# Seven products of a paced pair in two runs of matmuls, and a new order for ScalarE and VectorE

## The chip, the cores and the metric

The kernel runs on one core of one Trainium2 chip. The metric is device time in microseconds (us) of one execution, the median of several. Five engines of the core work side by side, each through its own list of instructions in order: TensorE (PE in the profile; its weight loads are listed apart as PEld), VectorE (DVE), ScalarE (ACT), GpSimd (POOL) and SyncE (SP, which only issues transfers here). They wait for one another by semaphores.

## What is computed

Two layers of a transformer on 512 tokens of width 1024, all in float32. Each layer has a feed-forward block, a token mixer, and a second feed-forward block, each followed by a layer norm. The change touches the first half of the feed-forward blocks only, of which there are four in the program:

```python
def _swiglu(x, w1, w2):
    gt, up = jnp.split(x @ w1, 2, axis=-1)
    return (jax.nn.silu(gt) * up) @ w2          # x: 512 x 1024, w1: 1024 x 5632, w2: 2816 x 1024

for l in range(DEPTH):                          # DEPTH = 2
    x = _layer_norm(DN_ALPHA * x + 0.5 * _swiglu(x, ffn1_w1[l], ffn1_w2[l]), ...)
    x = _layer_norm(DN_ALPHA * x + _token_mix(x, ...), ...)
    x = _layer_norm(DN_ALPHA * x + 0.5 * _swiglu(x, ffn2_w1[l], ffn2_w2[l]), ...)
```

`gt` and `up` have 2816 columns each, that is 22 blocks of 128. A **pair** is one such block of the gate columns with the same block of the up columns.

## The kernel before

**Split operands.** Every float32 operand stands as a high part (the value rounded to the type that TensorE multiplies in one pass) and a low part (the rest). A product is three matmuls: high by high, high by low, low by high. ScalarE makes the high part by a copy, VectorE the low part by a subtraction: lines 452 with `hi<-` and `lo<-` in the profile.

**Seven products.** Pairs 3 to 21 are computed by a scheme with seven half-size products in place of eight (Winograd's form), on sums of the tokens (tile `tz`, made once per block) and on sums of the weights (made for every pair). Pairs 4 to 21 go through `paced` (line 443), 18 iterations in each of the four blocks; these are the four **stages** of which this document speaks. Each product has contraction length 512, that is four steps of 128.

**sided** (line 411) issues products. Per product it issues four long matmuls (line 415: high weights by 512 columns, the high and low tokens side by side) and four short ones (line 418: low weights by 256 columns). Called with several products, it issues the long ones of all, then the short ones of all, these in reverse order if `back` is set. TensorE's order is that of the program text.

**The seven products of pair c, by letter** (weights in parentheses): P (`g1`) and Y (`g2`) use the two halves of the gate weights `ug`; D uses `ud`, the tile pair `dh`, `dl`; B (`ub`) and C (`uc`) use the two halves of the summed weights `u2`; A (`ua`) and E (`ue`) those of `u1`. P, B, A and E are summed one after the other in the PSUM bank `px`; D is summed into `pv`, Y into `py`, and C has `pc`. Between them stand copies by ScalarE: `px` after P goes to `py`, `px` after B to `pv`, `px` after A to the SBUF tile `cc`, and `px` after E, its second half, to `t`. Each copy must be done before the next product is added to `px`. VectorE then forms the up columns (`up`, line 505 and after: four additions on `cc` and `pv`), the gate columns (`gate`: two additions on `py` and `px`), ScalarE takes Silu of the gate, and VectorE multiplies the two.

**Weights of a pair.** `load` (line 470) fetches the raw gate and up columns, `rg` and `ru`, by SyncE. From them come `ug` = parts of `rg`; `dh`, `dl` = parts of the second half of `ru`; two sums in place in `ru` and in the tile `ws` (function `sums`); `u2` = parts of `ws`; `u1` = parts of `ru`. In the kernel before all of these are made for the **next** pair n, in the iteration of pair c.

**Order.** The helper `on` chains every instruction that `paced` gives to VectorE behind the one before it on VectorE, and the same on ScalarE. So each of the two engines takes the operations strictly in the order of the program text, and one that waits holds all behind it.

**Buffers.** `unit()` (line 143) hands out a pair of tiles `hi`, `lo` (1024 columns each), for `ug`, `u2` and `u1`. Successive calls go round a list of seven places in three pools; by the counter's value at the start of `paced` the pools come in the order wt, wt, wx, wx, w1p, w1p, wt, and again. The pool wt has three buffers, wx and w1p have two each. Within its pool a tile takes the buffer that came free first; where one alone is free or about to be, it takes that. It can be written only when the last reader of the buffer's former content is done. The same holds for the PSUM banks, which have four tags: `pc` and `px` of even iterations (counted from 0) share two banks; `px` of odd iterations and `pv` of even ones share two; `py` of even iterations has one; `pc`, `pv` and `py` of odd iterations share three.

Of the kernel before, what the change touches and what calls it, by code (L numbers as in the profile page):

```python
# [10 lines left out]
F32 = mybir.dt.float32  # L11
F32R = mybir.dt.float32r
BF = mybir.dt.bfloat16
AF = mybir.ActivationFunctionType
OP = mybir.AluOpType
# [4 lines left out]
P = 128  # L20
S, D, F = 512, 1024, 2816
KD, KF, NB = D // P, F // P, S // P
# [44 lines left out]
def body(tc, a, out, depth=DEPTH):  # L67
# [15 lines left out]
    def ps(tag=None, name="ps", shape=(P, 512)):  # L83
        if tag is None:
            tag = PS_ALL[ring[0] % 8]
            ring[0] += 1
        return psp.tile(list(shape), F32, name=name, tag=tag, bufs=PS_TAGS[tag])
# [29 lines left out]
    def wraw(shape=None):  # L117
        return wt.tile(list(shape or [P, KD, P]), F32, name="raw", tag="raw", bufs=3)
# [16 lines left out]
    def behind(*ins):  # L135

        st = ExitStack()
        for i in ins:
            if i:
                st.enter_context(tc.issue_after(i))  # L140
        return st

    def unit():

        if nx.pool:
            pl, nb = nx.pool, 4
        else:
            seq = [(wt, 3)] * 3 + [(more.pool, 2)] * 2 * bool(more.pool)
            if nx.w1:
                seq = seq[2:] + [(nx.w1, 2)] * 2 + seq[:2]  # L150
            more.n += 1
            pl, nb = seq[more.n % len(seq)]
        return [pl.tile([P, KD, P], F32R, name=n, tag=n, bufs=nb) for n in ("hi", "lo")]
# [193 lines left out]
    H1, H2 = slice(0, 256), slice(256, 512)  # L347
# [60 lines left out]
                nc.tensor.matmul(o, wx, vx, start=first and k == 0 and i == 0, stop=k == 3 and i == 2,  # L408
                                 skip_group_check=True)

    def sided(*ps_, back=False):
        for o, w, x, first in ps_:
            o = o.rearrange("p (z s) -> p z s", z=2)
            for k in range(4):
                nc.tensor.matmul(o, w[0][:, k], x[:, :, k], start=first and k == 0, stop=False, skip_group_check=True)  # L415
        for o, w, x, _ in reversed(ps_) if back else ps_:
            for k in range(4):
                nc.tensor.matmul(o[:, H1], w[1][:, k], x[:, 0, k], start=False, stop=k == 3, skip_group_check=True)  # L418

# [23 lines left out]
    def paced(w, c0, pl, tz, t2, hpart, fs, ws):  # L443

        last = {}
        V, A = nc.vector, nc.scalar

        def on(k, f, *args, **kw):  # L450
            with behind(last.get(k)), tc.high_priority(100):
                last[k] = f(*args, **kw).ins  # L452

        def tt(o, x, y, op=OP.add):
            on("v", V.tensor_tensor, o, x, y, op=op)

        def copy(o, x, f=AF.Copy):
            on("a", A.activation, o, x, f)

        def rest(lo, x, hi):  # L460
            tt(lo, x, hi.bitcast(F32), OP.subtract)

        v = w.rearrange("(k p) f -> p k f", p=P)
        h1, h2 = slice(0, 4), slice(4, 8)
        half = lambda u: [[y[:, h] for y in u] for h in (h1, h2)]
        two = lambda y: y.rearrange("p (z s) -> p z s", z=2)
        (t1, t2_, t3, t4) = [tz[:, i].rearrange("p k z s -> p z k s") for i in range(4)]
        p_, r_, s_ = [xx[:, :, k:k + 4, c] for k, c in ((0, H1), (4, H1), (4, H2))]

        def load(f):  # L470
            n = K()
            n.f, n.t, n.u = f, t2[:, f % 2], hpart(f)
            n.rg = wraw()
            nc.sync.dma_start(n.rg, v[:, :, f * P:f * P + P])
            n.ru = pl.tile([P, KD, P], F32, name="raw", tag="raw", bufs=2)
            nc.sync.dma_start(n.ru, v[:, :, c0 + f * P:c0 + f * P + P])
            return n

        def weights(n):
            n.dh, n.dl = [pl.tile([P, 4, P], F32R, name=x, tag=x, bufs=2) for x in ("dh", "dl")]  # L480
            n.wx = pl.tile([P, KD, P], F32, name="ws", tag="ws", bufs=1)
            n.ug, n.u2, n.u1 = unit(), unit(), unit()
            (a1, a2), (b1, b2) = half(n.u1), half(n.u2)
            n.ws = half(n.ug), (a2, b2, b1, a1), (n.dh, n.dl)

        def sums(n, i):
            if i == 0:
                rest(n.dl, n.ru[:, h2], n.dh)
                tt(n.ru[:, h2], n.ru[:, h1], n.ru[:, h2])
                rest(n.ug[1], n.rg, n.ug[0])  # L490
                g2 = n.rg[:, h1].rearrange("p k f -> p (k f)")[:, None].to_broadcast([P, 2, 512])
                tt(bk(n.wx), bk(n.ru), g2, OP.subtract)
            else:
                tt(n.ru[:, h1], n.rg[:, h2], n.wx[:, h2], OP.subtract)

        def gate(e, h, bank):
            tt(e.t[:, h], bank[:, H1], e.t[:, h])

        def up(e):
            m, side, c3 = e.cc[:, H1], e.cc[:, H2], e.cc[:, 512:768]  # L500
            tt(e.u[:, H2], m, side)
            tt(e.u[:, H1], e.pv[:, H1], c3)
            tt(e.u[:, H2], e.u[:, H2], c3)
            tt(e.u[:, H1], e.pv[:, H2], e.u[:, H1])

        bk = lambda y: y.rearrange("p (b k) f -> p b (k f)", b=2)
        fs = list(fs)
        c, e = K(), None
        c.f, c.t, c.u, c.ws = fs[0], t2[:, fs[0] % 2], hpart(fs[0]), ws
        n = load(fs[1])  # L510
        for _ in range(6):
            nc.vector.memset(ps(name="gap")[:, 0:1], 0.0)
        for f in fs:
            (g1, g2), (ua, ub, uc, _), ud = c.ws
            for x in (("pv", "py", "pc", "px"), ("pc", "pv", "py", "px"))[(f - fs[0]) % 2]:
                setattr(c, x, ps(name=x))
            first, b = (c.px, g1, p_, True), (c.px, ub, t2_, False)
            if e:
                copy(e.cc[:, 0:512], e.px)
            if e and e.f > fs[0]:  # L520
                sided((e.py, e.ws[0][1], r_, False), first, back=True)
            else:
                sided(first)
            if n:
                weights(n)
                copy(n.dh, n.ru[:, h2])
                copy(n.ug[0], n.rg)
                sums(n, 0)
            copy(c.py if e else c.t, c.px)
            if e:  # L530
                if e.f == fs[0]:
                    tt(e.t, e.py, e.t)
                    tt(e.t[:, H1], e.t[:, H1], e.t[:, H2])
                else:
                    copy(e.t[:, H1], e.py[:, H2])
                    gate(e, H1, e.py)
                sided((e.px, e.ws[1][3], s_, False), b, back=True)
            else:
                sided((c.py, g2, r_, True))
                sided(b)  # L540
            if n:
                sums(n, 1)
            copy(c.pv, c.px)
            if e:
                copy(e.t[:, H2], e.px[:, H2])
                up(e)
                gate(e, H2, e.px)
            sided((c.pc, uc, t3, True))
            if n:
                copy(n.u2[0], n.wx)  # L550
                rest(n.u2[1], n.wx, n.u2[0])
            if e:
                copy(e.t, e.t, AF.Silu)
                tt(e.u, e.t, e.u, OP.mult)
            if n:
                copy(n.u1[0], n.ru)
                rest(n.u1[1], n.ru, n.u1[0])
            c.cc = pl.tile([P, 1024], F32, name="cc", tag="cc", bufs=1)
            copy(c.cc[:, 512:768], c.pc[:, H2])
            tt(c.cc[:, 512:768], c.pc[:, H1], c.cc[:, 512:768])  # L560
            sided((c.pv, ud, t4, False), (c.px, ua, t1, False), back=True)
            e, c, n = c, n, load(f + 2) if f + 2 in fs else None
        copy(e.cc[:, 0:512], e.px)
        sided((e.py, e.ws[0][1], r_, False), (e.px, e.ws[1][3], s_, False))
        up(e)
        copy(e.t[:, H1], e.py[:, H2])
        gate(e, H1, e.py)
        copy(e.t[:, H2], e.px[:, H2])
        gate(e, H2, e.px)
        copy(e.t, e.t, AF.Silu)  # L570
        tt(e.u, e.t, e.u, OP.mult)
        return last["a"], last["v"]
# [1504 lines left out]
```

## Time and profile before

| what | us |
| --- | --- |
| median of three runs (2382.77 to 2385.82) | 2384.15 |
| the profiled execution's own time | 2385.5 |
| its span, from first to last instruction | 2383.5 |
| TensorE busy in the span | 2372.9 |
| VectorE busy | 2029.0 |
| ScalarE busy | 1380.6 |
| paced stages, from their first matmul on | 61.5 to 238.1, 910.1 to 1086.4, 1242.6 to 1418.9, 2090.6 to 2267.0 |

How to read a page: section 1 gives the busy time of each engine; section 4 follows the chain of work that ended last backwards, and gives its share by engine and line. The view by windows gives the busy time of each engine in a stretch. The timeline lists instructions in order: start, duration, engine, line, operation, out<-in, shapes, and in brackets the idle time just before it with the engine whose result ended it. Successive instructions of one engine overlap a little, so the distance between two starts, not the duration, is what one costs in a full queue. In the groups of four matmuls that the timeline merges, the distance from one group's start to the next is what the group costs.

### The profile page before, as it was taken

What the parts mean: (1) busy time and instruction counts of PE and PEld (TensorE: products, weight loads), DVE (VectorE), ACT (ScalarE), POOL (GpSimd) and SP (SyncE); (2) the same over time, 40 slices, a digit from 0 to 9 for tenths busy, and PEclk for the clock granted to TensorE, in tenths of its full rate; (3) what the DMA queues carried; (4) which work ended last, traced back from release to release, by engine and by line L of the source; (5) the groups of instructions that cost most, each with busy time, mean ns of one, the idle gap of its engine ahead of it and who ended that gap; (6) DMA issues with size and microseconds to landing.
All of it is one profiled execution on the core that took longest, in us unless ns stands there. A gap on an engine that the chain in (4) does not pass through costs nothing.

```text
span 2383.5 us, 38602 instructions
## 1 busy us (share of the span) xinstructions
PE 2372.9 (100%) x14017; PEld 2047.8 (86%) x14017; DVE 2029.0 (85%) x3974; ACT 1380.6 (58%) x2637; POOL 345.5 (14%) x598
## 2 busy tenths in 40 slices
PE   9999999999999999999999999999999999999998
PEld 8888888888889988888898888878888898888887
DVE  7999985787688889999799989667777888999996
ACT  4666644576644536666546666445766445466663
POOL 2000312133321000001100002122332210000021
PEclk9999999999999999999999999999999999999999
DMA  6433965633155353338833348645321654433394
GB/s 199 115 108 102 246 201 162 182 90 91 48 159 134 106 172 112 109 95 225 207 116 108 112 147 204 196 130 153 99 80 56 161 131 151 132 111 111 98 240 139
DMA packets 407933, 330.08 MB, mean 138 GB/s; under 512 B 19208, under 2 KB 349336, under 8 KB 407744
## 3 DMA queue, kind: packets, MB, share of 16 engines
q1 hardware_dynamic: 380752, 261.83, 37.0%
q0 software_dynamic: 26992, 65.80, 11.9%
q8 instruction: 110, 1.80, 0.3%
q14 instruction: 79, 0.65, 0.1%
HBM read 300.26 MB, written 17.88 MB: 133 GB/s over the span
## 4 chain that ended last, share of the span: by engine, by line
PE 99%; DMA 0%; DVE 0%; issue 0%; POOL 0%; SPq 0%; POOLq 0%; ACT 0%; DVEq 0%
PE acc L658 13%; PE px L415 11%; PE acc L195 7%; PE pj L181 6%; PE pj L183 6%; PE pj L182 6%; PE px L418 6%; PE pg L408 5%; PE py L415 3%; PE pv L415 3%; PE pc L415 3%; PE pu L408 2%; PE brp L181 2%; PE brp L182 2%; PE brp L183 2%; PE sN L1361 2%
## 5 line engine op out<-in xcount | busy, mean ns | idle before, releaser
L161 DVE TENSOR_TENSOR lo<-raw,hi 128x1024 fp32r<-128x1024 f32 x202 | 247.3, 1228 | 90.1 <-ACT hi L160 89.7
L160 ACT ACTIVATE hi<-raw 128x1024 fp32r<-128x1024 f32 x202 | 211.9, 1055 | 146.4 <-PE brp L182 36.3
L181 PE MATMUL pj<-xx,hi 128*128 128x512 f32 (+1 forms) x696 | 262.2, 377 | 1.8 <-ACT hi L1903 1.8
L183 PE MATMUL pj<-xx,lo 128*128 128x512 f32 (+1 forms) x696 | 251.0, 361 | 0.0
L182 PE MATMUL pj<-xx,hi 128*128 128x512 f32 (+1 forms) x696 | 250.7, 360 | 0.0
L658 PE MATMUL acc<-hi,xx 128*128 128x512 f32 x640 | 197.0, 389 | 0.0
L633 POOL DMA_DIRECT2D bt<-in_ffn_w_dram x32 | 40.3, 1266 | 924.7 <-DVE lo L161 712.3
L452 DVE TENSOR_TENSOR lo<-raw,hi 128x1024 fp32r<-128x1024 f32 x136 | 165.9, 1220 | 0.0
L415 PE MATMUL px<-tz,hi 128*128 128x512 f32 x576 | 156.8, 394 | 0.0
L415 PE MATMUL px<-xx,hi 128*128 128x512 f32 x576 | 156.0, 392 | 0.0
L183 PEld LDWEIGHTS pj<-xx,lo 128*128 128x128 f32 x696 | 131.9, 190 | 20.7 <-DVE lo L1904 0.2
L181 PEld LDWEIGHTS pj<-xx,hi 128*128 128x128 f32 x696 | 132.1, 190 | 17.8 <-issue 2.7
L182 PEld LDWEIGHTS pj<-xx,hi 128*128 128x128 f32 x696 | 132.4, 190 | 12.4 <-DVE xx L1989 0.2
L452 ACT ACTIVATE hi<-raw 128x1024 fp32r<-128x1024 f32 x136 | 142.6, 1048 | 0.1
L658 PEld LDWEIGHTS acc<-hi,xx 128*128 128x128 f32 x640 | 120.1, 188 | 25.0
L415 PEld LDWEIGHTS px<-tz,hi 128*128 128x128 f32 x576 | 107.2, 188 | 26.0 <-ACT py L452 2.3
L658 PE MATMUL acc<-lo,xx 128*128 128x512 f32 x320 | 124.5, 389 | 0.0
L415 PEld LDWEIGHTS px<-xx,hi 128*128 128x128 f32 x576 | 103.3, 189 | 18.2
L452 ACT ACTIVATE pv<-px 128x512 f32<-128x512 f32 x72 | 41.9, 582 | 124.7 <-PE px L418 124.7
L418 PEld LDWEIGHTS px<-tz,lo 128*128 128x128 f32 x576 | 88.1, 188 | 11.9
L418 PE MATMUL px<-xx,lo 128*128 128x256 f32 x576 | 92.0, 282 | 0.0
L418 PE MATMUL px<-tz,lo 128*128 128x256 f32 x576 | 91.3, 280 | 0.0
(490 smaller groups left out, 6776.9 us busy)
## 6 DMA issues: line engine op xcount, KB each, us to landing
raw<-in_ffn_w_dram SPq DMA_DIRECT2D x232, 512.0 KB, 3.9
raw<-in_w_in_dram SPq DMA_DIRECT2D x56, 512.0 KB, 4.1
raw<-in_w_gate_dram SPq DMA_DIRECT2D x48, 512.0 KB, 3.8
b<-in_ffn_w_dram SPq DMA_DIRECT2D x32, 512.0 KB, 6.7
bt<-in_ffn_w_dram POOLq DMA_DIRECT2D x32, 512.0 KB, 10.5
x_sp<-xa POOLq DMA_DIRECT2D x24, 512.0 KB, 6.1
xa<-x_sp POOLq DMA_DIRECT2D x24, 512.0 KB, 4.6
ks<-hl SPq DMA_DIRECT2D x96, 128.0 KB, 2.3
```

The costliest lines, as they stand in the source:

```text
L160: lnq.hi = nc.scalar.activation(hi[:, c], raw[:, c], AF.Copy).ins
L161: lnq.lo = nc.vector.tensor_tensor(lo[:, c], raw[:, c], hi[:, c].bitcast(F32), op=OP.subtract).ins
L181: nc.tensor.matmul(o, hi[:, k], vh, start=first, stop=False)
L182: nc.tensor.matmul(o, hi[:, k], vl, start=False, stop=False)
L183: nc.tensor.matmul(o, lo[:, k], vh, start=False, stop=last)
L195: nc.tensor.matmul(o, x(k)[:, t], y[:, c], start=first and i == 0, stop=last and i == 2, skip_group_check=True)
L408: nc.tensor.matmul(o, wx, vx, start=first and k == 0 and i == 0, stop=k == 3 and i == 2, skip_group_check=True)
L415: nc.tensor.matmul(o, w[0][:, k], x[:, :, k], start=first and k == 0, stop=False, skip_group_check=True)
L418: nc.tensor.matmul(o[:, H1], w[1][:, k], x[:, 0, k], start=False, stop=k == 3, skip_group_check=True)
L452: last[k] = f(*args, **kw).ins
L658: nc.tensor.matmul(o[t], u[:, k, s], v[:, c], start=first and j == 0 and i == 0, stop=False, skip_group_check=True)
L1361: nc.tensor.matmul(o[:, 0:nb].rearrange("p k b j -> p (k b j)"), q, kx[:, 2 * b0:2 * (b0 + nb)].rearrange("p a b -> p (a b)"), start=i == ...
```

## The change

`sided` takes for `back` the order in which the short matmuls are to follow. In an iteration there are now three pairs at work: c, the one before it e, and the one before that ee. From the third iteration on (index 2) TensorE issues two runs: the long matmuls of Y, D and A of e and of P of c (sixteen), then their short ones in the order A, P, D, Y; then the long ones of C of c, E of e and B of c (twelve), then the short ones in the order B, E, C. Before, there were four runs of eight, eight, four and eight long matmuls. Iterations 0 and 1 and the end of the loop have shorter forms.

The parts `u2` and `u1` are made for c in its own iteration, no longer for n in the one before; `ug`, `dh`, `dl` and the sums for n stay where the pair c is current. `unit()` is therefore called in each iteration for `ug` of n, `u2` of c and `u1` of c, in this order (iteration 0 only for `ug` of pair 1, and the last one only for `u2` and `u1`). The second half of the gate, Silu and the product of ee stand one iteration later than before.

VectorE's order in an iteration is now: gate of ee from `px`; the last sum of c; `lo` of `ug`; `lo` of `u2`; one addition on `cc` of e; `lo` of `u1`; the four additions of `up` of e; the product of ee; `dl` of n and a sum of n; gate of e from `py`; the sum in `ws` of n. ScalarE's is: `hi` of `ug`; copy `pc` to `cc` of e; `hi` of `u2`; `hi` of `u1`; Silu of ee; copy `px` to `cc` of e; copy `px` to `py` of c; copy `py` to `t` of e; `dh` of n; copy `px` to `pv` of c; copy `px` to `t` of e.

```diff
--- before.py
+++ after.py
@@ -408,12 +408,12 @@
                 nc.tensor.matmul(o, wx, vx, start=first and k == 0 and i == 0, stop=k == 3 and i == 2,
                                  skip_group_check=True)
 
-    def sided(*ps_, back=False):
+    def sided(*ps_, back=()):
         for o, w, x, first in ps_:
             o = o.rearrange("p (z s) -> p z s", z=2)
             for k in range(4):
                 nc.tensor.matmul(o, w[0][:, k], x[:, :, k], start=first and k == 0, stop=False, skip_group_check=True)
-        for o, w, x, _ in reversed(ps_) if back else ps_:
+        for o, w, x, _ in [ps_[i] for i in back] or ps_:
             for k in range(4):
                 nc.tensor.matmul(o[:, H1], w[1][:, k], x[:, 0, k], start=False, stop=k == 3, skip_group_check=True)
 
@@ -476,22 +476,32 @@
             nc.sync.dma_start(n.ru, v[:, :, c0 + f * P:c0 + f * P + P])
             return n
 
-        def weights(n):
-            n.dh, n.dl = [pl.tile([P, 4, P], F32R, name=x, tag=x, bufs=2) for x in ("dh", "dl")]
-            n.wx = pl.tile([P, KD, P], F32, name="ws", tag="ws", bufs=1)
-            n.ug, n.u2, n.u1 = unit(), unit(), unit()
-            (a1, a2), (b1, b2) = half(n.u1), half(n.u2)
-            n.ws = half(n.ug), (a2, b2, b1, a1), (n.dh, n.dl)
+        def parts(o, x):
+            copy(o[0], x)
+            rest(o[1], x, o[0])
 
         def sums(n, i):
             if i == 0:
+                n.dh, n.dl = [pl.tile([P, 4, P], F32R, name=x, tag=x, bufs=2) for x in ("dh", "dl")]
+                copy(n.dh, n.ru[:, h2])
                 rest(n.dl, n.ru[:, h2], n.dh)
                 tt(n.ru[:, h2], n.ru[:, h1], n.ru[:, h2])
-                rest(n.ug[1], n.rg, n.ug[0])
+            elif i == 1:
+                n.wx = pl.tile([P, KD, P], F32, name="ws", tag="ws", bufs=1)
                 g2 = n.rg[:, h1].rearrange("p k f -> p (k f)")[:, None].to_broadcast([P, 2, 512])
                 tt(bk(n.wx), bk(n.ru), g2, OP.subtract)
             else:
                 tt(n.ru[:, h1], n.rg[:, h2], n.wx[:, h2], OP.subtract)
+
+        def u2_parts(n):
+            n.u2 = unit()
+            parts(n.u2, n.wx)
+
+        def u1_parts(n):
+            n.u1 = unit()
+            parts(n.u1, n.ru)
+            (a1, a2), (b1, b2) = half(n.u1), half(n.u2)
+            n.ws = half(n.ug), (a2, b2, b1, a1), (n.dh, n.dl)
 
         def gate(e, h, bank):
             tt(e.t[:, h], bank[:, H1], e.t[:, h])
@@ -505,66 +515,95 @@
 
         bk = lambda y: y.rearrange("p (b k) f -> p b (k f)", b=2)
         fs = list(fs)
-        c, e = K(), None
+        def c_side(e):
+            e.cc = pl.tile([P, 1024], F32, name="cc", tag="cc", bufs=1)
+            copy(e.cc[:, 512:768], e.pc[:, H2])
+
+        def c_join(e):
+            tt(e.cc[:, 512:768], e.pc[:, H1], e.cc[:, 512:768])
+
+        def y_side(e):
+            if e.f > fs[0]:
+                copy(e.t[:, H1], e.py[:, H2])
+
+        def y_join(e):
+            if e.f > fs[0]:
+                gate(e, H1, e.py)
+            else:
+                tt(e.t, e.py, e.t)
+                tt(e.t[:, H1], e.t[:, H1], e.t[:, H2])
+
+        def prods(c):
+            (g1, g2), (ua, ub, uc, ue), ud = c.ws
+            return {"P": (c.px, g1, p_, True), "Y": (c.py, g2, r_, c.f == fs[0]), "B": (c.px, ub, t2_, False),
+                    "C": (c.pc, uc, t3, True), "D": (c.pv, ud, t4, False), "A": (c.px, ua, t1, False),
+                    "E": (c.px, ue, s_, False)}
+
+        c, e, ee = K(), None, None
         c.f, c.t, c.u, c.ws = fs[0], t2[:, fs[0] % 2], hpart(fs[0]), ws
         n = load(fs[1])
         for _ in range(6):
             nc.vector.memset(ps(name="gap")[:, 0:1], 0.0)
         for f in fs:
-            (g1, g2), (ua, ub, uc, _), ud = c.ws
             for x in (("pv", "py", "pc", "px"), ("pc", "pv", "py", "px"))[(f - fs[0]) % 2]:
                 setattr(c, x, ps(name=x))
-            first, b = (c.px, g1, p_, True), (c.px, ub, t2_, False)
+            if e is None:
+                sided(prods(c)["P"])
+                copy(c.t, c.px)
+            if ee:
+                gate(ee, H2, ee.px)
             if e:
+                sums(c, 2)
+            if n:
+                n.ug = unit()
+                parts(n.ug, n.rg)
+            if e:
+                c_side(e)
+                u2_parts(c)
+                c_join(e)
+                u1_parts(c)
+            if ee:
+                copy(ee.t, ee.t, AF.Silu)
+            q = prods(c)
+            if e:
+                r = prods(e)
+                if e.f > fs[0]:
+                    sided(r["Y"], r["D"], r["A"], q["P"], back=(2, 3, 1, 0))
+                else:
+                    sided(q["P"], r["D"], r["A"], back=(2, 0, 1))
                 copy(e.cc[:, 0:512], e.px)
-            if e and e.f > fs[0]:
-                sided((e.py, e.ws[0][1], r_, False), first, back=True)
-            else:
-                sided(first)
+                copy(c.py, c.px)
+                y_side(e)
+                up(e)
+            if ee:
+                tt(ee.u, ee.t, ee.u, OP.mult)
             if n:
-                weights(n)
-                copy(n.dh, n.ru[:, h2])
-                copy(n.ug[0], n.rg)
                 sums(n, 0)
-            copy(c.py if e else c.t, c.px)
             if e:
-                if e.f == fs[0]:
-                    tt(e.t, e.py, e.t)
-                    tt(e.t[:, H1], e.t[:, H1], e.t[:, H2])
-                else:
-                    copy(e.t[:, H1], e.py[:, H2])
-                    gate(e, H1, e.py)
-                sided((e.px, e.ws[1][3], s_, False), b, back=True)
-            else:
-                sided((c.py, g2, r_, True))
-                sided(b)
+                y_join(e)
             if n:
                 sums(n, 1)
+            if e:
+                sided(q["C"], r["E"], q["B"], back=(2, 1, 0))
+            else:
+                sided(q["Y"])
+                sided(q["C"], q["B"], back=(1, 0))
             copy(c.pv, c.px)
             if e:
                 copy(e.t[:, H2], e.px[:, H2])
-                up(e)
-                gate(e, H2, e.px)
-            sided((c.pc, uc, t3, True))
-            if n:
-                copy(n.u2[0], n.wx)
-                rest(n.u2[1], n.wx, n.u2[0])
-            if e:
-                copy(e.t, e.t, AF.Silu)
-                tt(e.u, e.t, e.u, OP.mult)
-            if n:
-                copy(n.u1[0], n.ru)
-                rest(n.u1[1], n.ru, n.u1[0])
-            c.cc = pl.tile([P, 1024], F32, name="cc", tag="cc", bufs=1)
-            copy(c.cc[:, 512:768], c.pc[:, H2])
-            tt(c.cc[:, 512:768], c.pc[:, H1], c.cc[:, 512:768])
-            sided((c.pv, ud, t4, False), (c.px, ua, t1, False), back=True)
-            e, c, n = c, n, load(f + 2) if f + 2 in fs else None
+            ee, e, c, n = e, c, n, load(f + 2) if f + 2 in fs else None
+        r = prods(e)
+        gate(ee, H2, ee.px)
+        c_side(e)
+        copy(ee.t, ee.t, AF.Silu)
+        c_join(e)
+        tt(ee.u, ee.t, ee.u, OP.mult)
+        sided(r["Y"], r["D"], r["A"], back=(2, 1, 0))
         copy(e.cc[:, 0:512], e.px)
-        sided((e.py, e.ws[0][1], r_, False), (e.px, e.ws[1][3], s_, False))
+        sided(r["E"])
+        y_side(e)
         up(e)
-        copy(e.t[:, H1], e.py[:, H2])
-        gate(e, H1, e.py)
+        y_join(e)
         copy(e.t[:, H2], e.px[:, H2])
         gate(e, H2, e.px)
         copy(e.t, e.t, AF.Silu)
```

## The prediction

> **What bounds the kernel now.** I read the page first: its span, its busy times and the chain that ended last. Then I read the view by windows over one paced stage.
>
> ```profile
> span 2383.5 us, 38602 instructions
> PE 2372.9 (100%) x14017; PEld 2047.8 (86%) x14017; DVE 2029.0 (85%) x3974; ACT 1380.6 (58%) x2637; POOL 345.5 (14%) x598
> PE 99%; DMA 0%; DVE 0%; issue 0%; POOL 0%; SPq 0%; POOLq 0%; ACT 0%; DVEq 0%
> ```
>
> ```profile
> 910.10:1086.40 176.30, 176.30 (x1009) 154.22 (x1008) 167.49 (x269) 116.11 (x194) 0.00 (x0) 1.00 0.36 107
> ```
>
> TensorE ends everything (99% of the chain). In a paced stage it is busy throughout, at a granted clock of 1.00; 18 iterations take 176.30 us, 9.79 us each. The third and fourth figures with a count are VectorE (167.49) and ScalarE (116.11): VectorE works 95% of the stage. So two things count here: what TensorE's own sequence costs, and whether VectorE, with half a microsecond to spare per iteration, still hands over in time. The timeline of TensorE, about one iteration, gives the first:
>
> ```profile
> 78.72 1.09 PE L415 MATMUL py<-xx,hi 128*128 128x512 f32 x4
> 79.65 1.07 PE L415 MATMUL px<-xx,hi 128*128 128x512 f32 x4
> 80.56 0.64 PE L418 MATMUL px<-xx,lo 128*128 128x256 f32 x4
> 81.03 0.64 PE L418 MATMUL py<-xx,lo 128*128 128x256 f32 x4
> 81.51 1.09 PE L415 MATMUL px<-xx,hi 128*128 128x512 f32 x4
> 82.48 0.76 PEld L415 LDWEIGHTS px<-tz,hi 128*128 128x128 f32 x4 [0.31 <-ACT py L452]
> 82.48 1.20 PE L415 MATMUL px<-tz,hi 128*128 128x512 f32 x4
> 83.52 0.63 PE L418 MATMUL px<-tz,lo 128*128 128x256 f32 x4
> 83.99 0.64 PE L418 MATMUL px<-xx,lo 128*128 128x256 f32 x4
> 84.46 1.09 PE L415 MATMUL pc<-tz,hi 128*128 128x512 f32 x4
> 85.39 0.63 PE L418 MATMUL pc<-tz,lo 128*128 128x256 f32 x4
> 85.86 1.09 PE L415 MATMUL pv<-tz,dh 128*128 128x512 f32 x4
> 86.79 1.09 PE L415 MATMUL px<-tz,hi 128*128 128x512 f32 x4
> 87.72 0.63 PE L418 MATMUL px<-tz,lo 128*128 128x256 f32 x4
> ```
>
> Distances of starts: a group of long matmuls costs 0.93 right after short ones (78.72 to 79.65), 0.91 as the second of a run (79.65 to 80.56); only A after D costs 0.93 again (86.79 to 87.72). A short group costs 0.47 right after long ones and 0.48 otherwise (81.03 to 81.51). So a change from short to long costs about 0.02, the change back returns 0.01. A waiting group costs its delay and about 0.1 on top: E at 82.48 came 0.04 late (81.51 + 0.93 = 82.44) and took 1.04 to the next group, not 0.91 to 0.93.
>
> VectorE, one iteration:
>
> ```profile
> 968.50 1.22 DVE L452 TENSOR_TENSOR lo<-raw,hi 128x1024 fp32r<-128x1024 f32 x1
> 969.64 1.22 DVE L452 TENSOR_TENSOR ws<-raw 128x1024 f32<-128x1024 f32 x1
> 970.77 0.42 DVE L452 TENSOR_TENSOR t<-py,t 128x256 f32<-128x256 f32 x1
> 971.11 0.68 DVE L452 TENSOR_TENSOR raw<-raw,ws 128x512 f32<-128x512 f32 x1
> 971.71 0.42 DVE L452 TENSOR_TENSOR ha<-cc 128x256 f32<-128x256 f32 x1
> 972.04 0.42 DVE L452 TENSOR_TENSOR ha<-pv,cc 128x256 f32<-128x256 f32 x1
> 972.38 0.41 DVE L452 TENSOR_TENSOR ha<-ha,cc 128x256 f32<-128x256 f32 x1
> 972.71 0.42 DVE L452 TENSOR_TENSOR ha<-pv,ha 128x256 f32<-128x256 f32 x1
> 973.04 0.41 DVE L452 TENSOR_TENSOR t<-px,t 128x256 f32<-128x256 f32 x1
> 973.45 1.23 DVE L452 TENSOR_TENSOR lo<-ws,hi 128x1024 fp32r<-128x1024 f32 x1
> 974.59 0.69 DVE L452 TENSOR_TENSOR ha<-t,ha 128x512 f32<-128x512 f32 x1
> 975.19 1.22 DVE L452 TENSOR_TENSOR lo<-raw,hi 128x1024 fp32r<-128x1024 f32 x1
> 976.33 0.42 DVE L452 TENSOR_TENSOR cc<-pc,cc 128x256 f32<-128x256 f32 x1
> 976.95 0.69 DVE L452 TENSOR_TENSOR dl<-raw,dh 128x512 fp32r<-128x512 f32 x1 [0.20 <-ACT dh L452]
> 977.68 0.69 DVE L452 TENSOR_TENSOR raw<-raw 128x512 f32<-128x512 f32 x1
> 978.29 1.22 DVE L452 TENSOR_TENSOR lo<-raw,hi 128x1024 fp32r<-128x1024 f32 x1
> ```
>
> The start distances price each step: 1024 columns 1.14, 512 columns 0.60 (`dl` 0.73, 976.95 to 977.68), 256 columns 0.33 to 0.34. In the new order, three steps precede `lo` of `u2`: 0.33 + 0.60 + 1.14 = 2.07. With it and the addition on `cc`, 3.54 precede `lo` of `u1`. From `lo` of `u1` to the end: 1.14 + 4 x 0.33 + 0.60 + 0.73 + 0.61 + 0.33 + 1.14 = 5.87. From `lo` of `u2`: 5.87 + 1.14 + 0.33 = 7.34. All: 9.41.
>
> **The change, part by part.**
>
> *Fewer changes between long and short.* Over a stage there are 126 long and 126 short groups before and after. Runs fall from 74 (five in iteration 0, four in each of 17, one at the end) to 39 (three, 34, two). That is 35 x 0.01, and A no longer pays its 0.02 in 18 places: 0.7 us. The small wait at E adds some 0.1 in a few places. I take 0.8 per stage, **3.2 us** for four. New iteration of TensorE: first run 0.93 + 3 x 0.91 + 0.47 + 3 x 0.48 = 5.58, second 0.93 + 2 x 0.91 + 0.47 + 2 x 0.48 = 4.18, together **9.76 us**. Bounds: nothing; or 1.6 us per stage, if every long group cost 0.91 and no wait were left.
>
> The Trainium skill's "TensorE: Matmul & The Clock Gate", section "Wait — 56ns, not 53.3ns?", gives a start distance of N / 2.4 GHz plus about 2.5 ns. That would be an estimated 0.86 for four long matmuls in any order, so regrouping would return nothing and the forecast would be 3 us higher. The trace has 0.91 and 0.93 by position, so I keep the saving.
>
> *Moved copies that nothing should feel.* All times now count from the start of the first run. A finished group of matmuls releases another engine about 0.2 after the next group starts (the short group at 83.52 ends at 84.15, the next began at 83.99). A's copy to `cc` starts at 4.3 and is done by 4.9, E wants it at 6.5. P's copy ends by 5.5, B wants the bank at 7.4. B's copy ends at 9.6, D of the next run wants it at 10.7. Each is covered by a group of other products. If that cover went, the price would be the 0.04 to 0.15 seen at E before. The removed stall at E is followed by nothing else on TensorE if VectorE is on time. Transfers: SyncE's load of `ru` two pairs on now waits for `u1` in the pair's own iteration, and the next `rg` queues behind it. It is issued by about 8 us, lands some 4 later, and is wanted at 15.8 or after. I cost it at nothing.
>
> *A buffer that comes free late.* This is where I expect the time. `u2` of c was made an iteration earlier; now `u2` and `u1` are made while e's `ug` is still needed, for Y of e stands in the first run and **its short matmuls end that run**. Seven pairs of buffers in pools of three, two and two, handed round three per iteration: in pool wx or w1p, when two units fall on it, one takes the idle buffer and the other the one with `ug` of e; in wt the third of three does. Counting places from `ug` of pair 1 in iteration 0, `u2` gets that buffer in iterations 3, 6, 9, 10, 13 and 16, `u1` in 4, 5, 8, 11, 12, 15 and 17; in 0, 1, 2, 7 and 14 neither does. So VectorE, which cannot go past a waiting step, stands until Y's last short matmul: 5.58 + 0.2 = 5.78. Queued behind it are `up`, the sums, the gate of e and at the iteration's end the next gate of ee. For the latter wait ScalarE's Silu and, because of the bank, TensorE.
>
> If **u1** waits, VectorE ends at 5.78 + 5.87 = 11.65, 1.89 into the next iteration. Its gate step (0.42 and 0.05 to release) is done at 2.36; P, fourth in the run, wants the bank at 0.93 + 2 x 0.91 = 2.75. No cost. If **u2** waits, VectorE ends at 5.78 + 7.34 = 13.12, 3.37 into the next. In an odd iteration `px` has the bank of ee's `px`, as the other one with its tag is e's `pv`; P gets it at 3.37 + 0.47 = 3.84, 1.09 late, and pays **1.19** with the restart. In an even one P gets the bank of ee's `pc`, long free, and C needs ee's at 5.58: no stop there. But ScalarE is late:
>
> ```profile
> 87.55 0.63 ACT L452 ACTIVATE t<-t 128x512 f32<-128x512 f32 x1 [1.54 <-DVE t L452]
> 88.09 1.04 ACT L452 ACTIVATE hi<-raw 128x1024 fp32r<-128x1024 f32 x1
> 89.03 0.36 ACT L452 ACTIVATE cc<-pc 128x256 f32<-128x256 f32 x1
> 89.30 0.59 ACT L452 ACTIVATE cc<-px 128x512 f32<-128x512 f32 x1
> ```
>
> `hi` of `u1` starts after the second VectorE step (3.37 + 0.33 + 0.68 + 0.05 = 4.43); Silu follows 0.94 later, the copy for E 0.54 after that (5.91), done 6.55: E, due at 6.50, pays 0.05 + 0.1 = **0.16**.
>
> Lateness passes on when the next iteration cannot drain it. After an unstopped even iteration, VectorE starts 2.86 late (3.37 + 9.41 - 9.76 - 0.16) and the following odd one pays 2.86 + 0.47 - 2.75 + 0.1 = 0.68; where the even one itself holds `u2` (10), it pays 3.21 + 0.47 - 2.75 + 0.1 = 1.03. Iterations 4 and 5: 0.16 + 0.68; 7: 1.19; 10 and 11: 0.16 + 1.03; 14 and 15: 0.16 + 0.68; 17: 1.19. Sum 5.25 per stage, **21.0 us** for four.
>
> Total: 2385.5 (the profiled execution, 2.0 more than its span) - 3.2 + 21.0 = 2403.3. The median lies 1.35 below that execution: **2402**.
>
> **Rivals.**
>
> *Nothing waits long enough.* The order pays as drawn: 2385.5 - 3.2 - 1.35 = 2381. For it: without the hold VectorE's 9.41 fit into 9.76, and TensorE's first dependence on the gate is 2.75 into the run. Against it: the hold leaves 7.34 + 0.47 of VectorE's work for 6.72 of TensorE's. If the two numbers crossed (1.1 less on VectorE), it would decide. Chance 0.16.
>
> *Each late gate stops P.* If `px` always had ee's bank, all six holds of `u2` would cost 1.19: 7.1 per stage, 2384.15 - 3.2 + 28.4 = 2409; if every `u1` hold added 0.3 for waits that I don't see, 2417. For it: VectorE is at 95%. Against it: the two banks with a common tag. Chance 0.2.
>
> *The buffers rotate strictly.* Then `u2` waits in every iteration from 3 on, each stops the next by about 1.1: 14 x 1.1 x 4 = 62, 2443. Against it: the pools hand out what came free. Chance 0.04.
>
> *Half the hold.* `u2` waits, but slack that I overlooked, 0.5 per stop, leaves 2.5 per stage: 2391. Chance 0.1.
>
> **How the numbers follow.** Forecast 0.5, own range 2395 to 2408. About 0.2% (4.8 us) is what a measurement of this kernel can tell from no change. Slower by more: forecast, second, third and last, 0.84. The first rival splits: within 0.2% 0.11, faster 0.05. The range 2387 to 2415 leaves out that rival, the strict rotation and the top of the second.
>
> **What would show it.** In the stage's windows iterations of about 9.8 and 10.4 to 10.9 alternate. VectorE's `lo<-ws` stands some 3 us behind PE `py` L418 six times per stage, `lo<-raw` up to 2 seven times; TensorE's load for `px<-xx` stands about 1 us behind VectorE's `t` three to six times. Undisturbed long groups at 0.91 in places 2 to 4 show the saving. I am wrong if `lo<-ws` never waits, or if TensorE's stops are released by ScalarE alone.

## The result, and the profile after

| | median of runs, us | runs | ratio to before |
| --- | --- | --- | --- |
| before | 2384.02 (2382.77 to 2385.82) | 6 | 1 |
| changed | 2401.69 (2400.81 to 2402.33) | 6 | 1.0073, interval 1.0060 to 1.0086 |

The change makes the kernel 17.7 us slower. The forecast was 2402.

First the page of the changed kernel: its span, its busy times, and the shares of the chain that ended last.

```profile
span 2400.6 us, 38805 instructions
PE 2378.2 (99%) x14017; PEld 2046.5 (85%) x14017; DVE 2026.6 (84%) x3974; ACT 1375.6 (57%) x2637; POOL 343.3 (14%) x598
...
PE 12%; DVE 2%; issue 0%; POOL 0%; POOLq 0%; DVEq 0%
```

The same 14017 matmuls are there, and no engine got more work. But the chain now steps from TensorE to VectorE and back; before, it ran through TensorE alone (99%). It could be followed back only to 2055 us, shortly before the last stage, so its shares add up to some 14% of the span and say nothing of the rest. The stage itself says more. This is the view by windows over the second stage (length, then PE, PEld, DVE and ACT busy, granted clock, share and rate of transfers):

```profile
912.20:1093.30 181.10, 177.94 (x1010) 154.18 (x1009) 167.90 (x269) 116.41 (x197) 0.00 (x0) 1.00 0.35 104
```

The stage took 176.30 before, with TensorE busy for all of it. Now it takes 181.10. TensorE stands idle for 3.2 of that (181.10 - 177.94), and its busy time grew by 1.6: groups that start late, or restart more slowly after a wait, without showing as idle. From the first matmul to the last one's end the four stages add up to 706.8 us before and 725.3 after: 18.5 more. The spans differ by 1.4 less (17.1): the changed kernel's first stage began 2.5 earlier, at 59.05 and not 61.51, and some 1.0 of that was lost again between the stages, most of it between the third and the fourth. The head start arose in the first microseconds of the program, which the change doesn't touch (last section).

Where in the stage? TensorE's timeline over iteration 3, which nothing stops, and the first run of iteration 7:

```profile
935.94 1.09 PE L415 MATMUL py<-xx,hi 128*128 128x512 f32 x4
936.87 1.07 PE L415 MATMUL pv<-tz,dh 128*128 128x512 f32 x4
937.78 1.07 PE L415 MATMUL px<-tz,hi 128*128 128x512 f32 x4
938.69 1.07 PE L415 MATMUL px<-xx,hi 128*128 128x512 f32 x4
939.60 0.64 PE L418 MATMUL px<-tz,lo 128*128 128x256 f32 x4
...
941.51 1.09 PE L415 MATMUL pc<-tz,hi 128*128 128x512 f32 x4
...
945.69 1.09 PE L415 MATMUL py<-xx,hi 128*128 128x512 f32 x4
...
975.88 1.09 PE L415 MATMUL py<-xx,hi 128*128 128x512 f32 x4
976.81 1.07 PE L415 MATMUL pv<-tz,dh 128*128 128x512 f32 x4
977.72 1.07 PE L415 MATMUL px<-tz,hi 128*128 128x512 f32 x4
979.79 1.20 PE L415 MATMUL px<-xx,hi 128*128 128x512 f32 x4 [0.99 <-DVE t L452]
980.82 0.63 PE L418 MATMUL px<-tz,lo 128*128 128x256 f32 x4
```

The first run takes 5.57 (935.94 to 941.51), the second 4.18 (to 945.69): 9.75 us, where the prediction had 9.76. The last five lines are the first run of iteration 7. Its fourth group, P (`px<-xx,hi`), starts 2.07 behind the third and not 0.91: it is 1.16 late, and its four matmuls take 1.03 instead of 0.91 after the wait. The releaser is VectorE's `t`, the gate of ee.

The timeline of VectorE just before shows where that lateness begins:

```profile
971.97 1.23 DVE L452 TENSOR_TENSOR lo<-ws,hi 128x1024 fp32r<-128x1024 f32 x1 [1.71 <-PE py L418]
973.12 0.42 DVE L452 TENSOR_TENSOR cc<-pc,cc 128x256 f32<-128x256 f32 x1
973.45 1.22 DVE L452 TENSOR_TENSOR lo<-raw,hi 128x1024 fp32r<-128x1024 f32 x1
...
978.18 1.22 DVE L452 TENSOR_TENSOR ws<-raw 128x1024 f32<-128x1024 f32 x1
979.31 0.42 DVE L452 TENSOR_TENSOR t<-px,t 128x256 f32<-128x256 f32 x1
```

In iteration 6 `lo` of `u2` (`lo<-ws`) stands still for 1.71 until Y's last short matmul is done: the next group begins at 971.70, `lo` at 971.97. From there VectorE runs without a gap, and 7.34 later (979.31) it reaches the gate on which P waits. By then TensorE is 3.43 into iteration 7; P was due at 2.75.

Counted this way, as the excess of each run over 5.57 and 4.18, the second stage has these stops, in us:

| iteration | 4 | 5 | 7 | 10 | 11 | 14 | 15 | 16 | 17 | sum |
| --- | --- | --- | --- | --- | --- | --- | --- | --- | --- | --- |
| predicted | 0.16 | 0.68 | 1.19 | 0.16 | 1.03 | 0.16 | 0.68 | 0 | 1.19 | 5.25 |
| measured | 0.29 | 0.66 | 1.27 | 0.30 | 0.97 | 0.25 | 0.68 | 0.34 | 0.93 | 5.69 |

All other iterations are calm. The view of waits over the stage (engine and line, its releaser, us in all, times, longest) sums them up:

```profile
...
ACT hi L452 <- DVE ws L452: 22.3, 15, 2.6
DVE lo L452 <- PE py L418: 8.0, 8, 1.7
PEld px L415 <- DVE t L452: 5.2, 5, 1.4
...
PEld px L415 <- ACT cc L452: 1.7, 4, 0.5
```

Eight holds of VectorE, six at `lo<-ws` and two at `lo<-raw` (a ninth, of 0.91 at `lo<-raw` in 17, is put down to ScalarE's `py`, but ends where the others do, 0.27 behind the start of the group that follows Y's short matmuls); five loads of P's weights behind VectorE's gate, in 5, 7, 11, 15 and 17; four of E's behind ScalarE's copy to `cc`, in 4, 10, 14 and 16: the nine stops of the table. ScalarE's 22.3 us behind `ws` is mostly idleness that costs nothing by itself: it is the sign that VectorE is the late one.

### The profile page after: what moved, and what is told of

Its sections match the earlier page's. It is cut to its first block, busy times and chain, and to the rows that moved or that the text cites. A ratio compares the mean times of both kernels' runs of the same rounds, so it can differ in the third digit from the quotient of the medians.

```text
span 2400.6 us, 38805 instructions
## 1 busy us (share of the span) xinstructions
PE 2378.2 (99%) x14017; PEld 2046.5 (85%) x14017; DVE 2026.6 (84%) x3974; ACT 1375.6 (57%) x2637; POOL 343.3 (14%) x598
## 5 line engine op out<-in xcount | busy, mean ns | idle before, releaser
L181 PEld LDWEIGHTS pj<-xx,hi 128*128 128x128 f32 x696 | 131.9, 189 | 16.6 <-issue 2.7
L452 ACT ACTIVATE hi<-ws 128x1024 fp32r<-128x1024 f32 x68 | 72.2, 1061 | 89.2 <-DVE ws L452 89.2
L452 DVE TENSOR_TENSOR lo<-ws,hi 128x1024 fp32r<-128x1024 f32 x68 | 83.1, 1222 | 30.1 <-PE py L418 29.3
```

The costliest lines, as they stand in the source:

```text
L181: nc.tensor.matmul(o, hi[:, k], vh, start=first, stop=False)
```

## The experiments

Theory: VectorE's hold before `lo` of `u2`, caused by the way in which `unit()` hands buffers round, makes the gate late, and the bank that P shares with ee's gate hands this on to TensorE. Rivals: VectorE is simply too full in the new order; the long runs are slow in themselves; the buffers' holds are harmless and something else stops P. Each edit is against the changed kernel; each ratio is against the kernel before on the same chip (2382.99 for the first four, 2383.1 for the others).

**e1, buffers by kind.** Each kind of tile gets buffers of its own from the same three pools, so that no `u2` or `u1` meets a `ug` that is still read.

```diff
+        def own(p, nb):
+            more.n += 1
+            return [p.tile([P, KD, P], F32R, name=x, tag=x, bufs=nb) for x in ("hi", "lo")]
-            n.u2 = unit()
+            n.u2 = own(more.pool, 2)
-            n.u1 = unit()
+            n.u1 = own(nx.w1, 2)
-                n.ug = unit()
+                n.ug = own(wt, 3)
```

> Buffers by kind, as many as before: ug from wt (three), u2 from wx (two), u1 from w1p (two). Then neither u2 nor u1 ever falls on the buffer of the ug that Y still reads; order of all engines as in the changed kernel. Theory (the late buffer is the cause): VectorE's lo<-ws no longer waits for py L418, TensorE no longer waits for t, the 5.7 us of stops per stage go, 2401.7 - 4 x 5.7 = 2379, that is some 4 us under the kernel before. Rival (VectorE's new order is too full by itself, 9.4 of 9.76 us per iteration): the stops stay, 2396 to 2402. Rival (long runs of matmuls are slow in themselves): 2399 to 2402.

Measured: 2380.76 (2380.55 to 2382.36), ratio 0.9991 (0.9982 to 1.0000), 1.8 above the 2379 expected: some 2 us of small stops are left in the four stages. The view of waits over its second stage has no row with `lo` behind PE `py` left, and this in place of the 5.2 above:

```profile
PEld px L415 <- DVE t L452: 0.6, 2, 0.5
```

The whole loss is gone, with the same runs, the same order and the same work on VectorE. VectorE is not too full and the long runs are not slow. The four stages add up to 704.6, 2.2 less than before.

**e2, Y's short matmuls first.** The buffers stay as they are, but the reader of the held one ends about 1.4 earlier.

```diff
-                    sided(r["Y"], r["D"], r["A"], q["P"], back=(2, 3, 1, 0))
+                    sided(r["Y"], r["D"], r["A"], q["P"], back=(0, 2, 3, 1))
```

> In the first run the short matmuls of Y stand first in place of last; buffers as in the changed kernel. Theory: the buffer of ug comes free 1.43 us earlier, VectorE held by u2 ends 1.9 us into the next iteration in place of 3.4, the gate is done at 2.4 and P wants the bank at 2.75, so nearly all stops go: 2379 to 2382. lo<-ws may still wait for py L418, but harmlessly. Rival (VectorE too full): 2396 to 2402, and up waits longer for D, which now ends the run. Rival (long runs slow): 2399 to 2402.

Measured: 2382.60 (2382.28 to 2383.29), ratio 0.9998 (0.9989 to 1.0007), a little above the expected range. The timeline of VectorE in iteration 6:

```profile
964.74 1.23 DVE L452 TENSOR_TENSOR lo<-ws,hi 128x1024 fp32r<-128x1024 f32 x1 [0.96 <-PE py L418]
```

VectorE is still held in four iterations of the second stage (6, 9 and 13 for about 0.95, 10 for 0.26), but until 4.40 into the iteration and no longer until 5.84, and in iterations 2 to 15 this stops nothing; only in 16 and 17 does TensorE stop, for 0.35 and 0.63. In the changed kernel a hold of only 0.26, in iteration 10, is followed by a stop of 0.97. So the length of the hold is not the matter, but when it ends.

**e3, another bank for P in odd iterations.** This was meant to keep the hold and take P out of ee's bank.

```diff
-            for x in (("pv", "py", "pc", "px"), ("pc", "pv", "py", "px"))[(f - fs[0]) % 2]:
+            for x in (("pv", "py", "pc", "px"), ("px", "pv", "py", "pc"))[(f - fs[0]) % 2]:
```

> In odd iterations px and pc change their places in the ring of PSUM banks, so that P of an odd iteration gets a bank that came free in the iteration before. The hold of VectorE by the buffer stays. Theory: VectorE is as late as in the changed kernel (lo<-ws still waits for py L418), P never waits for the gate; the stops of 0.7 to 1.3 us in odd iterations go, those of about 0.3 us at E, behind ScalarE, stay or become a little more: some 1.8 us per stage in place of 5.7, about 2386. Rival (VectorE too full): 2396 to 2402. If instead the bank has no part in it: 2401.

Measured: 2401.20 (2401.03 to 2401.74), ratio 1.0076 (1.0062 to 1.0089). A miss, and its stage has the waits of the changed kernel to the digit:

```profile
...
DVE lo L452 <- PE py L418: 8.0, 8, 1.7
PEld px L415 <- DVE t L452: 5.2, 5, 1.4
...
PEld px L415 <- ACT cc L452: 1.7, 4, 0.5
```

The edit had not done what it was meant to do. In the addresses of the built program `px` of the odd iterations stands in one and the same bank throughout, as it does in the changed kernel, though its tag now had three: P got ee's bank again. The run says nothing on the theory, but it shows that the order of the names within an iteration does not settle the bank, and that "takes the buffer that came free first" is not enough to tell which bank a tile gets.

**e4, a hold in every iteration.** `u2` and `ug` share the three buffers of one pool, so that `u2` meets e's `ug` each time from iteration 2 on.

```diff
-            n.u2 = unit()
+            n.u2 = own(*(wt, 3) if n.f > fs[1] else (more.pool, 2))
-            n.u1 = unit()
+            n.u1 = own(more.pool, 2)
-                n.ug = unit()
+                n.ug = own(wt, 3)
```

> The dose raised: ug and u2 both from wt (three buffers; in iteration 1 u2 from wx), u1 from wx, so that u2 falls on the buffer of the ug that Y still reads in every iteration from 2 or 3 on, where it was six of eighteen. Theory: lo<-ws waits for py L418 in each of these; odd iterations pay 0.9 to 1.2 us at P, even ones about 0.3 us at E: 9.5 us per stage in place of 5.7, 2417 (2412 to 2422). Rival (VectorE too full by itself) and rival (long runs slow): no change from 2401.7.

Measured: 2420.11 (2419.57 to 2420.43), ratio 1.0154 (1.0140 to 1.0168). The cost grows with the number of holds: six of `u2` per stage cost 21 us over e1, 15 cost 39. In the trace every odd iteration stops at P (1.27 for the first, 0.97 for each after it) and every even one from 4 on at E (0.30): about 10.2 per stage. The waits, and one of VectorE's rows:

```profile
...
DVE lo L452 <- ACT py L452: 10.7, 7, 1.5
PEld px L415 <- DVE t L452: 9.2, 8, 1.4
...
DVE lo L452 <- PE py L418: 3.2, 8, 1.4
PEld px L415 <- ACT cc L452: 3.1, 7, 0.4
```

```profile
946.99 1.09 PE L415 MATMUL pc<-tz,hi 128*128 128x512 f32 x4
...
947.26 1.23 DVE L452 TENSOR_TENSOR lo<-ws,hi 128x1024 fp32r<-128x1024 f32 x1 [1.52 <-ACT py L452]
```

Eight holds are put down to PE `py`, seven to ScalarE's `py`. But each of the seven ends 0.27 behind the start of the group that follows Y's short matmuls (946.99 to 947.26), just as 971.70 to 971.97 above. The releaser's name is inferred; the place where the wait ends tells more.

**e5, P's bank by turns.** The hold stays. In odd iterations `px` is drawn from two tags by turns, so that it does not stand in ee's bank.

```diff
-            for x in (("pv", "py", "pc", "px"), ("pc", "pv", "py", "px"))[(f - fs[0]) % 2]:
+            for x in (("pv", "py", "pc", "px"), ("pc", "pv", "py", "px"),
+                      ("pv", "py", "pc", "px"), ("px", "pv", "py", "pc"))[(f - fs[0]) % 4]:
```

> The same question as the third run, which left px of odd iterations on one bank throughout: now every second odd iteration takes its px from the other group of banks, so that P of an odd iteration gets the bank of the pc before it, free an iteration earlier. The hold of VectorE by the buffer stays as in the changed kernel. Theory: lo<-ws still waits for py L418 six times per stage, TensorE no longer waits for VectorE's t at P; left are stops of about 0.3 us at E, behind ScalarE's cc, in some six iterations per stage: 4 x 1.8 over the run with buffers by kind (2380.8), about 2388 (2385 to 2391). If the bank has no part in it: 2401.

Measured: 2385.12 (2384.28 to 2385.56), ratio 1.0008 (0.9999 to 1.0017). This is what e3 was to test: in the addresses of this program `px` of the odd iterations takes two banks by turns. VectorE is still held in all six places (five by the row below; the sixth, in iteration 3, is put down to ScalarE's `py` and ends at the same place), and P no longer stops; the row with `t` is gone, and what is left are E's small stops behind ScalarE, 0.23 to 0.37 in five iterations:

```profile
...
DVE lo L452 <- PE py L418: 4.2, 5, 1.3
...
PEld px L415 <- ACT cc L452: 2.1, 5, 0.5
```

So the hold makes VectorE late, and the shared bank carries it to TensorE. Without the second link 16.6 of the 20.9 us between the changed kernel and e1 go.

**e6, e1 and e5 together.** Both edits as above.

> Buffers by kind as in the first run, and banks as in the run with px apart. No hold, and no bank that comes free late. Theory: what is left in the first run of a stop at P late in the stages (0.3 us per stage) goes too: 2379.5 to 2381, against 2380.8 there. Rival (VectorE too full): nothing gained over 2380.8, or lost.

Measured: 2380.99 (2380.47 to 2381.98), ratio 0.9992 (0.9983 to 1.0001). Nothing over e1: the stop of P in iteration 17 is gone, but E stops there instead, for 0.24.

**e7, `u1` held instead of `u2`.** `u2` never meets `ug`; `u1` does in every iteration from 2 on.

```diff
+        def chain(j):
+            return own((more.pool, nx.w1)[j % 4 // 2], 2)
-            n.u2 = unit()
+            n.u2 = own(wt, 3)
-            n.u1 = unit()
+            n.u1 = chain(n.f - fs[0] - 1)
-                n.ug = unit()
+                n.ug = chain(n.f - fs[0])
```

> The other dose: u2 gets buffers of its own in wt, and u1 falls on the buffer of the ug that Y still reads in every iteration from 2 on (four rotating buffers in wx and w1p). So VectorE is held in sixteen iterations per stage, but before lo of u1, with 5.87 us of work behind it in place of 7.34. Theory: lo<-raw waits for py L418 in every iteration, VectorE ends 1.9 us into the next one, the gate is done at 2.4 and P wants the bank at 2.75: no stop, 2380 to 2383. Rival (every hold costs, whatever stands behind it): sixteen holds against six, 2410 or more.

Measured: 2383.22 (2382.62 to 2385.01), ratio 1.0001 (0.9992 to 1.0010), just above the expected range: E stops for 0.77 in iteration 17 (the row with `cc`). Thirteen holds behind PE `py` in the stage, in iterations 4 to 16 and not in sixteen, but more than the eight of the changed kernel, and none of them stops P:

```profile
...
DVE lo L452 <- PE py L418: 3.3, 13, 0.3
...
PEld px L415 <- ACT cc L452: 0.9, 1, 0.9
```

VectorE's timeline from the hold in iteration 4 to the gate for which P of the next iteration waits:

```profile
947.12 1.23 DVE L452 TENSOR_TENSOR lo<-raw,hi 128x1024 fp32r<-128x1024 f32 x1 [0.26 <-PE py L418]
...
952.99 0.42 DVE L452 TENSOR_TENSOR t<-px,t 128x256 f32<-128x256 f32 x1
```

Again it is the buffer of the `ug` that Y reads, and the hold ends at the same place, 5.84 into the iteration; but 5.87 us of VectorE's work stand behind `lo` of `u1` (947.12 to 952.99) and 7.34 behind `lo` of `u2`. In e4 holds just as short, 0.26 in the even iterations, are followed by stops of P of 0.97. That difference of 1.47 is what sets 2383 here apart from 2420 in e4, which holds `u2` about as often.

**e8, four runs instead of two.** e1's buffers and order, with TensorE's products split up again.

```diff
-                    sided(r["Y"], r["D"], r["A"], q["P"], back=(2, 3, 1, 0))
+                    sided(r["Y"], r["D"], back=(1, 0))
+                    sided(r["A"], q["P"])
-                sided(q["C"], r["E"], q["B"], back=(2, 1, 0))
+                sided(q["C"])
+                sided(r["E"], q["B"], back=(1, 0))
```

> Buffers by kind as in the first run, but the matmuls of an iteration in four runs again (Y D, A P, C, E B) in place of two; the orders of VectorE and ScalarE as in the changed kernel. What the fewer changes between long and short matmuls are worth by themselves: two more changes per iteration at 0.01 to 0.02 us each, 0.35 to 0.7 us per stage, so 2382 to 2383.5 against 2380.8. Rival (the start distance of a matmul does not depend on its neighbours): 2380.8.

Measured: 2383.24 (2382.54 to 2384.54), ratio 1.0002 (0.9993 to 1.0011). Against e1 the two runs are worth 2.5 us by the medians, and 2.3 by the stages (706.9 against 704.6); against e6, which ran on the same chip but has e5's banks, 2.3 by the medians, with no overlap of the two ranges. The windows of the second stage, first of e1, then of e8:

```profile
906.20:1082.30 176.10, 175.94 (x1010) 154.79 (x1009) 169.91 (x270) 117.31 (x197) 0.00 (x0) 1.00 0.36 107
```

```profile
907.10:1083.90 176.80, 176.61 (x1010) 154.70 (x1010) 169.25 (x270) 115.93 (x197) 0.00 (x0) 1.00 0.36 107
```

TensorE is busy for nearly all of both stages; it does the same matmuls in 0.7 less.

## Why the prediction was right

**The bound.** Right: in an undisturbed iteration TensorE's own sequence sets the time, and VectorE gets through in 9.75 us when nothing holds it (e1). The rival in which the order pays as drawn (2381) is e1's time; it was not the kernel's because the hold was real.

**The saving of the regrouping.** Predicted 0.8 per stage and 3.2 in all, of which 0.7 per stage are the regrouping itself. That part was right: without its stops the changed kernel's four stages take 702.6 (725.3 - 22.8), and those of before, without theirs, 705.4, which is 2.8 less; the new iteration takes 9.75 against the 9.76 worked out. The rest was too small: the stops of the kernel before, mostly at E in iterations 1 and 2, are 1.4 in the four stages, not 0.1 per stage. e8 against e1 measures 2.3 to 2.5; both keep about as much in stops, 0.65 each in their second stage: in iteration 1 P's load is 0.3 late (VectorE comes late to the loop from the work before it), and in iteration 17 VectorE runs steps of the phase after the stage. The Trainium skill, "TensorE: Matmul & The Clock Gate", section "Wait — 56ns, not 53.3ns?", gives one distance of starts for each width, N / 2.4 GHz plus about 2.5 ns, and names no dependence on what stands ahead; by that e8 would have equalled e1. Here the measurement decides: groups of four long matmuls cost 0.91 or 0.93 by position, and regrouping pays.

**The moved copies and the load of `ru`.** Costed at nothing: e1 contains all of them and is no slower than before.

**The hold: place and mechanism right, its length wrong.** `lo<-ws` is held in exactly the predicted 3, 6, 9, 10, 13 and 16. But "some 3 us" was too long. In the timeline of VectorE:

```profile
941.78 1.23 DVE L452 TENSOR_TENSOR lo<-ws,hi 128x1024 fp32r<-128x1024 f32 x1 [1.70 <-PE py L418]
...
992.74 1.23 DVE L452 TENSOR_TENSOR lo<-raw,hi 128x1024 fp32r<-128x1024 f32 x1 [0.40 <-PE py L418]
...
1012.24 1.23 DVE L452 TENSOR_TENSOR lo<-ws,hi 128x1024 fp32r<-128x1024 f32 x1 [0.26 <-PE py L418]
```

The holds last 1.7 four times and about 0.25 twice. `lo<-raw` waits in only three of the seven iterations named, 0.40 in 8, 0.25 in 12 and 0.91 in 17, not "up to 2 us" in seven; in the addresses of the built program `u1` does fall on e's `ug` in all seven, but in the other four VectorE reaches that step when the buffer is already free. The prediction worked out each hold as if VectorE had entered the iteration on time; it came out of the one before already late (by some 2 us in iteration 3, before any hold), so less was left to wait. The sum did not suffer, because it was counted from where the hold ends, not from its length: 5.78 predicted, 5.84 measured (0.27 after the next group's start, not 0.2), then 7.34 to the gate, exactly as in the rows of before.

**The stop of P.** Predicted 1.19, measured 1.27 in iteration 7 (gate at 3.43 for 3.37; 0.12 for the restart, not 0.1). The passed-on stops are close: 0.66, 0.97 and 0.68 for 0.68, 1.03 and 0.68. Iteration 17 has 0.93 for 1.19: iteration 16 had already stopped 0.34.

**The stop of E.** Right in cause, but worked out at little more than half its size: 0.16 for 0.25 to 0.30. These are rows of iteration 4 from the timeline of all engines:

```profile
949.24 1.06 ACT L452 ACTIVATE hi<-ws 128x1024 fp32r<-128x1024 f32 x1 [2.15 <-DVE ws L452]
...
951.72 0.57 ACT L452 ACTIVATE cc<-px 128x512 f32<-128x512 f32 x1
...
952.34 0.76 PEld L415 LDWEIGHTS px<-xx,hi 128*128 128x128 f32 x4 [0.42 <-ACT cc L452]
```

`hi` of `u2` waits 2.15 for VectorE's `ws`, and all of ScalarE's copies behind it are late. The copy for E was worked out to start at 5.91; it starts 6.03 into the iteration (951.72 - 945.69), and E's weights load at 6.65, where E was due at 6.50. The restart adds the rest.

**Missed.** Iteration 16 stops 0.34. VectorE there takes a step that is not of the stage, and waits for ScalarE ahead of it:

```profile
1067.33 1.23 DVE L161 TENSOR_TENSOR lo<-raw,hi 128x1024 fp32r<-128x1024 f32 x1 [0.40 <-ACT hi L160]
```

It is a weight's low part for the next phase, 1.6 us with its wait, on an engine with about 0.3 to spare per iteration. The trace of before was read for one stage's own steps only.

**The bank.** The step "`px` has the bank of ee's `px`" held, in the trace and in the addresses, and e5 shows that it is the link. P stops in odd iterations only, which rules out the rival in which every late gate stops it. The reason given for it, which tiles share its tag, did not carry over to e3: with three banks in its tag `px` still kept one. What picks the bank stays open.

**The sum.** Predicted + 21.0 - 3.2; measured in the four stages 22.8 of stops (4 x 5.69), 18.5 net, so 4.2 on the other side: 2.8 from the regrouping and 1.4 of stops that before has and the new order hasn't. Both terms came out about 1 to 2 us larger and offset each other. That the total fell within 0.3 us of the forecast is partly luck.

**The best version.** e1 keeps the change's order and gives each kind of tile its own buffers: 2380.76, about 2 us under the kernel before, with an interval that just touches no difference, and 21 us under the changed kernel.

## What to carry to other kernels

When buffers of several kinds are handed round one ring and the time of one kind's making moves, work out for every place of the ring who still reads the old content; give each kind its own buffers if the sizes allow it. Price a hold on an in-order engine by where it ends plus the work queued behind it up to the step that another engine needs (here 7.34 hurt and 5.87 did not), not by how long the engine waits. And look for the shared bank or buffer by which lateness reaches the bound engine: taking that link away (e5) recovered some four fifths of the loss with VectorE still held.

## What had not been expected of the hardware

The profiled execution of the kernel before lost some time at its very start. The windows from 9 to 12 us (granted clock third from the end), of before and of after:

```profile
9.00:12.00 3.00, 2.86 (x13) 2.70 (x14) 1.43 (x4) 1.00 (x4) 0.00 (x0) 0.58 1.06 385
```

```profile
9.00:12.00 3.00, 3.00 (x28) 3.00 (x28) 1.39 (x4) 1.48 (x4) 0.00 (x0) 1.00 1.07 385
```

After an idle gap of 1.84 us (ended by ScalarE's `hi` at 9.14) the clock granted to TensorE was 0.58 in these three microseconds and 0.63 from 12.0 to 13.2, and matmuls of 256 columns started 0.21 apart instead of 0.12. In the profiles of the nine other kernels the clock there was 1.00, with gaps at the same place of 0.54 to 1.59. Against the changed kernel these matmuls began 1.0 later (9.14 and 8.13), and the first one behind the twelve slow ones and the eight transposes that follow them 2.5 later (13.18 and 10.68). This is the head start of 2.5 with which the changed kernel's first stage began: 1.0 from the later start, 1.5 while the clock was low. Whether the length of the gap decides, and which length is tolerated, can't be told from one case.
